# New step tables for the token mixers of a decoder layer, and tail copies on two engines

## The chip, the cores and the metric

The kernel runs on one core of a Trainium2 chip. Its engines work side by side, each through its own list of instructions in order: TensorE (PE in the profile, its weight loads PEld), VectorE (DVE), ScalarE (ACT), GpSimd (POOL) and SyncE (SP), which issues the DMAs here. The metric is the device time of one execution in microseconds. Before the change it is 2779.05 us, the median of three runs (2774.12, 2779.05 and 2781.64).

## The reference

One decoder layer on 2048 tokens of width 1024, in float32. An input projection feeds two groups of token mixers, and the rest is an output projection, a squared-ReLU MLP and a gated embedding:

```python
proj = jnp.einsum('btd,dc->btc', rms_norm(h, pre_mix_norm), w_in)
qkv = jax.nn.silu(causal_depthwise_conv(qkv, gdn_conv))          # q, k, v of 4 heads
o_a = gated_delta_rule_chunked(l2norm(q_a), l2norm(k_a), v_a, g_dec, beta)
o_a = gated_head_norm(o_a, gdn_norm, z_gdn)
o_b = hgrn2_chunked(jax.nn.silu(q_hg), k_b, i_hg, log_f)         # 4 more heads
o_b = gated_head_norm(o_b, hgrn_norm, g_hg)
h = h + rms_norm(concat(o_a, o_b) @ w_out, post_mix_norm)
y = jnp.square(jax.nn.relu(rms_norm(h, pre_mlp_norm) @ w_mlp_up)) @ w_mlp_down
h = h + rms_norm(y, post_mlp_norm)
e = rms_norm(p @ w_ple_proj, ple_norm)
h = h + e * jax.nn.sigmoid(h @ w_ple_gate)
```

Inside the gated delta rule each chunk needs a triangular system solved: with k the keys and decay the running gates, `a_mat = I + strict_lower((beta k) k^T * decay)`, then `u = a_mat^-1 (beta v)` and `w = a_mat^-1 (beta k exp(gc))`. The state runs from chunk to chunk.

## The kernel before

The 2048 tokens are cut into four quarters of 512. Large products are done as three float32r products of a split into a high and a low part, so one output tile of the input projection is 24 matmuls of 128x512.

**Works and steps.** The mixer stage (about 46 to 1136 us) is a list of 132 works: in each quarter one work for the decay inputs (`ab`) and 8 per head for 4 heads (k, q, v and z of the delta rule, then f, i, q and g of HGRN2). A work is 24 matmuls and is cut into three steps of 8. After each step `tick()` runs one piece of every mixer whose turn it is: a mixer is a generator, and a table of offsets (`A_STEPS` for the delta rule, `B_STEPS` for HGRN2, `A_LAST` and `B_LAST` for the very last head) says at which steps after its head's start each of its pieces, from `yield` to `yield`, is emitted. A head starts every 24 steps and its mixers take some 60, so the pieces of two or three heads lie between the matmuls of a third.

**What sets the order.** On TensorE and SyncE the order is the order of emission (`manual_schedule`). On VectorE, ScalarE and GpSimd a scheduler orders the instructions when the program is built. All engines take their lists in order, and wait for each other by semaphores. A work's split weights are kept in DRAM in quarter 0 and reloaded by SyncE in the later quarters; the reload waits until TensorE has left the buffer, which ties SyncE's place to TensorE's.

**The delta rule's pieces** (`gdn_mixer`), in their order: the decays' load (`gf`); their exponentials (`e`); the keys turned, their squares summed (`ssk`, L598) and `ktail`; the root (L602, on GpSimd); the scales `cc`, `ncc`, `inv` (L606); the products `kk` (L621, L622), the system `u` (L625), `qk`, and the keys and queries scaled by the decays (L629 to L631); the values turned, and the store of the system, `ud` (L641, four DMAs); its load in another layout, `sys` (L650), with the off-diagonal blocks (`um`); the inverse of the 32-wide blocks by substitution in eight pieces on VectorE (L656 to L666); its store `xd` and load `xt` (L671, L678); a transpose on VectorE (`xn`, L680); the combination to 128 wide (`psp`, `psx`, `pst`, `psd`, L685); then the recurrence, three pieces for each of four chunks: `psa` (L727) and `r` (L729), `psb` (L732) and `w` (L734), `psc` (L737), the output and the new state `S` (L739). In it TensorE and VectorE alternate from step to step.

**The head's end** (`finish`, `norm_steps`): squares, a sum over partitions on TensorE (`nrm`, L262), that row copied by ScalarE (L265) and stored by SyncE in the same piece (`sd`, L267), loaded again in another layout (L270), scaled and rooted (L272, L158), stored (`rd`, L276), loaded over all partitions (`rsb`, L237), multiplied into `og` (L556) and stored (`mixd`, L558).

**HGRN2's pieces** (`hgrn_mixer`): elementwise products, six levels (L801 to L829; each with products `at`, masked copies and scaled queries and keys), and a recurrence of four chunks (L841 to L845).

**Between the quarters** `decays` turns the work `ab` into decays (L462 to L486, with transposes `ps_gb` at L482), `load_x` loads, scales and splits the next quarter's x (L943 to L959), and `down_sums` (L979 to L990) prepares sums of MLP weights on VectorE.

**The tail.** When the works are done, at about 1088 us, 16 tiles of the embedding's projection (`embed_tile`, 6 matmuls each, `mme`) fill TensorE between the last mixers' pieces. Each tile lies in one of two banks of `pm`; ScalarE copies it (`e`, L299) and squares it (`sq_e`, L225), VectorE adds the squares (L226), SyncE stores the copy (L301).

## Time and profile before

| | us |
|---|---|
| median of three runs | 2779.05 |
| the profiled execution | 2779.64 |
| its span, first to last instruction | 2777.8 |
| TensorE busy | 2694.8 (97%) |
| VectorE busy | 2045.8 (74%) |
| ScalarE busy | 1470.1 (53%) |
| TensorE's granted clock | 0.994 |

In the stretch from 140 to 560 us TensorE is busy for 406.04 of 420 us and VectorE for 326.16; from 1050 to 1135 us for 76.33 and 65.55 of 85 us. In a row of a group, the number behind the bar is the busy time, then the mean of one instruction in ns, then the idle time just before the group's instructions with what ended it. In a row of the waits stand who waited for whom, the total in us, the number of times, and the longest. A row of the timeline has the start, the duration, engine, line and operation, and in brackets the idle time before it. SPq is SyncE's queue of DMA issues. Quarters and heads are counted from 0.

### The profile page before, as it was taken

What the parts mean: (1) busy time and instruction counts of PE and PEld (TensorE: products, weight loads), DVE (VectorE), ACT (ScalarE), POOL (GpSimd) and SP (SyncE); (2) the same over time, 40 slices, a digit from 0 to 9 for tenths busy, and PEclk for the clock granted to TensorE, in tenths of its full rate; (3) what the DMA queues carried; (4) which work ended last, traced back from release to release, by engine and by line L of the source; (5) the groups of instructions that cost most, each with busy time, mean ns of one, the idle gap of its engine ahead of it and who ended that gap; (6) DMA issues with size and microseconds to landing.
All of it is one profiled execution on the core that took longest, in us unless ns stands there. A gap on an engine that the chain in (4) does not pass through costs nothing.

```text
span 2777.8 us, 38374 instructions
## 1 busy us (share of the span) xinstructions
PE 2694.8 (97%) x12721; PEld 2216.6 (80%) x12721; DVE 2045.8 (74%) x4242; ACT 1470.1 (53%) x2943; POOL 103.8 (4%) x104
## 2 busy tenths in 40 slices
PE   7999999999999999999899999999999999999999
PEld 5788788788888887777688888887888888887887
DVE  6787877777777677577889767857787765567765
ACT  6665555455546445576555546545455445465421
POOL 0000000000000000000000000001000000001000
PEclk9999999999999999999999999999999999999999
DMA  7777777667666665887466447667454356677663
GB/s 261 261 246 221 238 235 245 218 208 252 216 212 201 213 226 169 274 278 256 139 216 221 170 168 245 220 195 237 160 189 153 139 171 204 194 254 242 216 200 122
DMA packets 268598, 589.24 MB, mean 212 GB/s; under 512 B 55642, under 2 KB 59960, under 8 KB 249200
## 3 DMA queue, kind: packets, MB, share of 16 engines
q1 hardware_dynamic: 268400, 586.79, 63.4%
q8 instruction: 101, 1.65, 0.3%
q14 instruction: 97, 0.79, 0.1%
HBM read 419.75 MB, written 166.92 MB: 211 GB/s over the span
## 4 chain that ended last, share of the span: by engine, by line
PE 58%; DVE 13%; DMA 9%; issue 6%; ACT 3%; SPq 1%; POOL 1%; DVEq 0%; POOLq 0%; ACTq 0%
PE u L1091 22%; PE d L1091 19%; PE mm L1023 7%; PE mmg L1091 6%; DVE pr_g L661 2%; DMA ud_g<-u_g 2%; DVE xs_g L664 1%; DMA sys_g<-ud_g 1%; DVE xs_g L666 1%; PE mmo L1091 1%; DMA rd_g<-m_g 1%; DMA da<-sumd 1%; DMA rsb_g<-rd_g 1%; DMA raw_xt<-in_xT_dram 1%; DMA b<-h1d 1%
## 5 line engine op out<-in xcount | busy, mean ns | idle before, releaser
L1023 PE MATMUL mm<-xt,w 128*128 128x512 f32 x3072 | 775.1, 401 | 2.3 <-DVE acc_vg L505 0.8
L1023 PEld LDWEIGHTS mm<-xt,w 128*128 128x128 f32 x3072 | 560.5, 189 | 113.0 <-DVE acc_vg L505 1.3
L1091 PE MATMUL d<-db,da 128*128 128x512 f32 x2688 | 614.1, 390 | 6.3 <-ACT db L215 4.0
L1091 PE MATMUL u<-t,wu 128*128 128x512 f32 x2604 | 608.1, 396 | 3.3 <-ACT wu L162 3.3
L1091 PEld LDWEIGHTS d<-db,da 128*128 128x128 f32 x2688 | 505.1, 188 | 114.6 <-ACT db L215 5.3
L1091 PEld LDWEIGHTS u<-t,wu 128*128 128x128 f32 x2604 | 489.7, 188 | 121.0 <-ACT wu L162 4.1
L216 DVE TENSOR_TENSOR db<-db 128x512 fp32r<-128x512 f32 x224 | 160.5, 717 | 77.0 <-ACT db L215 75.8
L1420 DVE TENSOR_TENSOR u<-u,u 128x512 f32<-128x512 f32 x224 | 150.3, 682 | 73.2 <-PE u L1091 72.0
L215 ACT ACTIVATE db<-db 128x512 fp32r<-128x512 f32 x224 | 140.8, 629 | 86.1 <-DMA db<-hid 84.1
L1091 PE MATMUL mmo<-mixT,w_out 128*128 128x512 f32 x720 | 172.5, 400 | 8.7 <-DVE w_out L163 6.3
L1091 PE MATMUL mmg<-h2T,wg 128*128 128x512 f32 x768 | 178.2, 394 | 0.0
L1461 ACT ACTIVATE u<-u 128x512 f32<-128x512 f32 x128 | 80.9, 632 | 179.0 <-DVE u L1420 178.6
L1091 PEld LDWEIGHTS mmo<-mixT,w_out 128*128 128x128 f32 x720 | 137.1, 191 | 43.1 <-DVE w_out L163 8.1
L1091 PEld LDWEIGHTS mmg<-h2T,wg 128*128 128x128 f32 x768 | 144.4, 188 | 33.5
L163 DVE TENSOR_TENSOR da<-da 128x512 fp32r<-128x512 f32 x128 | 93.8, 732 | 86.9 <-ACT da L162 86.5
L162 ACT ACTIVATE da<-da 128x512 fp32r<-128x512 f32 x128 | 80.4, 628 | 135.3 <-DMA da<-sumd 100.9
L162 ACT ACTIVATE wu<-a 128x512 fp32r<-128x512 f32 x124 | 74.1, 624 | 49.1 <-DMA a<-in_w_up_dram 47.9
L661 DVE TENSOR_TENSOR pr_g<-xs_g,sys_g 128x16 f32<-128x16 f32 (+14 forms) x240 | 93.8, 391 | 5.3
L226 POOL TENSOR_TENSOR acc_y<-acc_y,sq_y 128x512 f32<-128x512 f32 x28 | 38.2, 1363 | 1398.0 <-ACT sq_y L225 1398.0
L163 DVE TENSOR_TENSOR wu<-a,wu 128x512 fp32r<-128x512 f32 x124 | 84.7, 686 | 4.8 <-ACT wu L162 4.6
L1462 ACT ACTIVATE u<-u 128x512 f32<-128x512 f32 x128 | 80.8, 631 | 3.7
L163 DVE TENSOR_TENSOR da<-dr,da 128x512 fp32r<-128x512 f32 x96 | 66.2, 689 | 16.0 <-ACT da L162 13.6
(374 smaller groups left out, 3802.2 us busy)
## 6 DMA issues: line engine op xcount, KB each, us to landing
w<-cache_in SPq DMA_DIRECT2D x96, 1024.0 KB
db<-hid SPq DMA_DIRECT2D x224, 256.0 KB
cache_in<-w SPq DMA_DIRECT2D x32, 1024.0 KB
hid<-u SPq DMA_DIRECT2D x128, 256.0 KB
da<-sumd SPq DMA_DIRECT2D x128, 256.0 KB
a<-in_w_up_dram SPq DMA_DIRECT2D x124, 256.0 KB
hid<-ht SPq DMA_DIRECT2D x96, 256.0 KB
dr<-in_w_down_dram SPq DMA_DIRECT2D x96, 256.0 KB
```

Source lines behind the costliest of these rows:

```text
L162: S.activation(t[:, 0], raw, AF.Copy)
L163: eng.tensor_tensor(t[:, 1], raw, t[:, 0], ALU.subtract)
L215: S.activation(t[:, 0], plain(t), AF.Copy)
L216: V.tensor_tensor(t[:, 1], plain(t), t[:, 0], ALU.subtract)
L226: eng.tensor_tensor(acc, acc, sq, ALU.add)
L661: V.tensor_tensor(pr[:, :, :, 0:i], xs[:, None, :, 0:i].broadcast_to([P, 2, GC, i]), sys[:, 0:i, i : i + 2].rearrange("p j two -> p two j" ...
L664: V.tensor_reduce(xs[:, :, i : i + 2].rearrange("p g two -> p two g"), pr[:, :, :, 0 : i + 1], AX.X, ALU.add)
L1023: PE.matmul(ps, *terms[i], start=i == 0, stop=i == nt - 1)
L1091: PE.matmul(ps, a, b, start=start, stop=stop)
L1420: V.tensor_tensor(c[new], c[old], ps, ALU.add)
L1461: S.activation(c[k], c[k], AF.Relu)
L1462: S.activation(c[k], c[k], AF.Square)
```

## The change

All instructions stay the same in kind and number, but for eight copies that move from ScalarE to VectorE, and two more loads of ScalarE's function tables (70 for 68). The tables of offsets change:

- In `gdn_mixer` the store `ud` gets a piece of its own directly behind `kk`, `u` and the scaled keys; the turned values follow in the next piece. The piece of the root comes two steps behind the squares instead of one. Counted from the head's start, kk goes from step 10 to 11, the store stays at 12, the load `sys` goes from 14 to 15, the inverse from 16 to 17, and everything behind it one step later.
- In `norm_steps` the store `sd` is a piece of its own, one step behind the row's copy. The tables of all callers get one more entry.
- The last head of the first three quarters runs its pieces from the store `xd` on three steps later still; head 0 of quarter 0 runs all its pieces two steps later.
- `load_x` of quarters 2 and 3 starts 16 steps before the quarter instead of 9.
- `decays` has 7 in place of 5 as its fourth offset in quarter 0.
- In the tail `e` is copied by VectorE for odd tiles.

```diff
-A_STEPS = ((3, 6, 7, 8, 9, 10, 12, 14) + tuple(range(16, 24)) + (24, 26, 28, 30, 32, 34, 36)
-           + tuple(range(38, 50)) + (50, 52, 54, 56, 57, 58, 60, 61))
+A_STEPS = ((3, 6, 7, 9, 10, 11, 12, 13, 15) + tuple(range(17, 25)) + (25, 27, 29, 31, 33, 35, 37)
+           + tuple(range(39, 51)) + (51, 53, 54, 56, 58, 59, 61, 63, 64))
-B_STEPS = (24, 26, 28, 30, 32, 34, 36, 38, 40, 42, 43, 44, 45, 46, 48, 50, 52, 53, 54, 56, 57)
+B_STEPS = (24, 26, 28, 30, 32, 34, 36, 38, 40, 42, 43, 44, 45, 46, 48, 49, 51, 53, 54, 56, 58, 59)
-A_LAST = (A_STEPS[:16] + (24, 25, 27, 28, 29, 30, 31) + tuple(range(32, 44))
-          + (44, 46, 48, 49, 50, 51, 53, 54))
-B_LAST = tuple(range(24, 38)) + (39, 41, 42, 43, 44, 46, 47)
+INVERSE = 17
+A_LAST = ((3, 6, 7, 8, 9, 10, 11, 12, 14) + tuple(range(16, 24)) + (24, 25, 27, 28, 29, 30, 31)
+          + tuple(range(32, 44)) + (44, 46, 47, 49, 50, 51, 52, 54, 55))
+B_LAST = tuple(range(24, 38)) + (39, 40, 42, 43, 44, 46, 48, 49)
...
         S.activation(row, ps[0:1, :], AF.Copy)
+        yield
         sd = dr.tile([1, QT], F32, name=f"sd_{name}")
         nc.sync.dma_start(sd, row)
         yield
...
-        S.activation(e, ps, AF.Copy)
+        if turns and d % 2:
+            V.tensor_copy(e, ps)
+        else:
+            S.activation(e, ps, AF.Copy)
...
             yield
-            psv = turned(live.pop("v"), f"v{n}", pp)
-            vt = mt(f"vt_{n}", "vt", 2)
-            S.activation(flat(vt), psv, AF.Copy)
 
             ud = dr.tile([NC, NB, SB, SB], F32, name=f"ud_{n}")
             for b in range(NB):
                 sl = slice(b * SB, (b + 1) * SB)
                 nc.sync.dma_start(ud[:, b].rearrange("c j i -> j c i"), u[sl, :, sl])
+            yield
+            psv = turned(live.pop("v"), f"v{n}", pp)
+            vt = mt(f"vt_{n}", "vt", 2)
+            S.activation(flat(vt), psv, AF.Copy)
             yield
...
+                if h == 3 and q < NQ - 1:
+                    a_steps = a_steps[:INVERSE] + tuple(o + 3 for o in a_steps[INVERSE:])
+                if h == q == 0:
+                    a_steps = tuple(o + 2 for o in a_steps)
...
-            at(per_q * q, load_x(q), range(-9, 0))
+            at(per_q * q, load_x(q), range(-9, 0) if q == 1 else (-16, -14, -12, -10, -8, -6, -3, -2, -1))
...
-               [4 * q + i for i in (0, 2, 4, 5, 6)])
+               [4 * q + i for i in (0, 2, 3, 5, 6, 7)])
...
-                        at(clock[0], decays(ps, q), (0, 2, 4, 5))
+                        at(clock[0], decays(ps, q), (0, 2, 4, 5 if q else 7))
...
-                    new = embed_tile(q, d, ple[d // 4], pts[q], accs, m2, 2)
+                    new = embed_tile(q, d, ple[d // 4], pts[q], accs, m2, 2, True)
...
-                           [1 + i for i in (0, 2, 4, 5, 6)])
+                           [1 + i for i in (0, 2, 3, 5, 6, 7)])
```

Three places show what the tables do to the lists. In the names g1_1 is the delta rule of quarter 1, head 1, h1_0 HGRN2 of quarter 1, head 0; the last number is the buffer's, and it and the line numbers differ between the two programs. The first place is VectorE around the system of head 1 in quarter 1; before, and then after:

```order
L822 TENSOR_TENSOR qk_h1_0_3757<-qk_h1_0_3757,gg_h1_0_3_4248 128x2x8x16
L823 COPY_PREDICATED att_h1_0_4026<-cst_84,at_h1_0_4_4294 128x2x8x16
L818 TENSOR_TENSOR qk_h1_0_3757<-qk_h1_0_3757,gg_h1_0_5_4370 128x2x2x64
L625 SCALAR_TENSOR_TENSOR u_g1_1_4306<-kk_g1_1_0_4308,ncc_g1_1_4196,e_g1_1_3875 128x128 x2
L628 TENSOR_TENSOR qk_g1_1_4307<-kk_g1_1_0_4308,e_g1_1_3875 128x256
L556 SCALAR_TENSOR_TENSOR og_g0_3_3995<-og_g0_3_3995,cols_87,rsb_g0_3_4191 128x512
L625 SCALAR_TENSOR_TENSOR u_g1_1_4306<-kk_g1_1_2_4316,ncc_g1_1_4196,e_g1_1_3875 128x128 x2
L628 TENSOR_TENSOR qk_g1_1_4307<-kk_g1_1_2_4316,e_g1_1_3875 128x256
```

```order
L829 TENSOR_TENSOR qk_h1_0_3730<-qk_h1_0_3730,gg_h1_0_3_4230 128x2x8x16
L830 COPY_PREDICATED att_h1_0_4006<-cst_84,at_h1_0_4_4279 128x2x8x16
L996 TENSOR_TENSOR wd2_0_4164<-wd2_1_4165,wd2_0_4164 128x512
L825 TENSOR_TENSOR qk_h1_0_3730<-qk_h1_0_3730,gg_h1_0_5_4359 128x2x2x64
L997 TENSOR_TENSOR wd2_1_4165<-wd2_1_4165,wd2_0_4164 128x512
L631 SCALAR_TENSOR_TENSOR u_g1_1_4314<-kk_g1_1_0_4316,ncc_g1_1_4187,e_g1_1_3851 128x128 x2
L634 TENSOR_TENSOR qk_g1_1_4315<-kk_g1_1_0_4316,e_g1_1_3851 128x256
L631 SCALAR_TENSOR_TENSOR u_g1_1_4314<-kk_g1_1_2_4324,ncc_g1_1_4187,e_g1_1_3851 128x128 x2
L634 TENSOR_TENSOR qk_g1_1_4315<-kk_g1_1_2_4324,e_g1_1_3851 128x256
```

The output of an earlier head (og_g0_3) no longer stands between the two halves of u, and the weight sums (wd2, down_sums) now stand ahead of u instead of behind it.

The second place is SyncE's queue from a weight reload ahead of the store to the load of the same system; before, and then after:

```order
L183 DMA w_24_1_1_4344<-cache_in25_1634 128x2048
L641 DMA ud_g1_1_4379<-u_g1_1_4306 32x4x32 x4
L431 DMA xs2_2_1_4394<-in_x_dram 128x512
L650 DMA sys_g1_1_4424<-ud_g1_1_4379 128x1x1024
L183 DMA w_28_1_1_4433<-cache_in29_1732 128x2048
```

```order
L185 DMA w_24_1_1_4340<-cache_in25_1614 128x2048
L644 DMA ud_g1_1_4361<-u_g1_1_4314 32x4x32 x4
L239 DMA rsb_g0_3_4376<-rd_g0_3_4305 128x512
L437 DMA xs2_2_1_4392<-in_x_dram 128x512
L185 DMA w_28_1_1_4418<-cache_in29_1712 128x2048
L657 DMA sys_g1_1_4441<-ud_g1_1_4361 128x1x1024
```

The load of the system has moved behind the next weight reload (w_28), and the load of an earlier head's scale (rsb_g0_3) now stands between store and load.

The third place is TensorE early in quarter 1, where the last head of quarter 0 goes on (psp5_g0_3) and the decays of quarter 1 are turned (ps_gb_1); before, and then after:

```order
L1023 MATMUL mm_0_1_0_3400<-xt1_2_3163,w_0_1_0_3235 128x512 x2
L685 MATMUL psp5_g0_3_3413<-xn_g0_3_3307,um5_553 128x128 x2
L816 MATMUL at_h0_3_2_3420<-qk_h0_3_2953,keys_h0_3_1_3369 128x2x64 x2
L482 MATMUL ps_gb_1_3434<-cst_84,gb_1_3314 128x36
L482 MATMUL ps_gb_1_3434<-cst_84,gbb_1_3432 128x36
```

```order
L1034 MATMUL mm_8_1_0_3473<-xt1_5_3194,w_8_1_0_3312 128x512
L692 MATMUL psp5_g0_3_3507<-xn_g0_3_3402,um5_553 128x128 x2
L823 MATMUL at_h0_3_4_3514<-qk_h0_3_2938,keys_h0_3_3_3457 128x2x64 x2
L541 MATMUL t_kg1_0_3529<-cst_84,y_kg1_0_3385 128x128 x4
L1034 MATMUL mm_8_1_0_3473<-xt1_5_3194,w_8_1_0_3312 128x512 x2
```

The piece psp5_g0_3 has gone from the second work of the quarter behind its first step (mm_0) to the third work behind its second (mm_8), four steps later; the transposes ps_gb stay in mm_0, in quarter 1 as in quarter 0.

More of the change, by code (lines that the diff above doesn't have):

```diff
@@ L292, in stage_ple, with embed_tile @@
         return ready
-    def embed_tile(q, d, w, pt, accs, pool, bufs):
+    def embed_tile(q, d, w, pt, accs, pool, bufs, turns=False):
         ps = bank(f"mme_{q}_{d}")
```

## The prediction

> **What bounds the kernel now.** I read the page first, then the waits of TensorE and SyncE's queue, then the timeline around the largest of these waits. The page:
>
> ```profile
> span 2777.8 us, 38374 instructions
> PE 2694.8 (97%) x12721; PEld 2216.6 (80%) x12721; DVE 2045.8 (74%) x4242; ACT 1470.1 (53%) x2943; POOL 103.8 (4%) x104
> L1023 PE MATMUL mm<-xt,w 128*128 128x512 f32 x3072 | 775.1, 401 | 2.3 <-DVE acc_vg L505 0.8
> ```
>
> TensorE is busy for 97% of the span, and the change takes no matmul away. What it can win is idle time of TensorE alone, 2777.8 - 2694.8 = 83 us in all, and of that the part that lies in the mixer stage. The big projection of that stage hardly waits (2.3 us over 3072 matmuls). The waits sit at the small matmuls of the mixers:
>
> ```profile
> PE psb_g L732 <- DVE r_g L729: 16.6, 19, 2.5
> PE mme L189 <- ACT sq_e L225: 12.6, 8, 5.4
> PE psp_g L685 <- DVE xn_g L680: 3.7, 4, 1.6
> PE psa_g L727 <- DVE S_g L739: 3.5, 5, 1.1
> PE ps_gb L482 <- DVE gbb L479: 2.8, 1, 2.8
> PE ps_gb L482 <- DVE gb L472: 1.4, 1, 1.4
> ```
>
> The columns are total us, times, longest. All but the mme rows wait for VectorE, so the question is why VectorE is late. It runs its list in order, and the lists of waits show what holds it and what holds SyncE's queue (140 to 1050 us):
>
> ```profile
> DVE xs_g L666 <- DMA sys_g<-ud_g: 20.2, 8, 3.7
> SPq L650 <- DMA ud_g<-u_g: 48.7, 15, 6.0
> SPq L267 <- ACT osq_h L265: 51.6, 13, 5.0
> SPq L267 <- ACT osq_g L265: 36.1, 14, 4.3
> ```
>
> VectorE stands 20.2 us, in 8 heads, before the first instruction of the triangular inverse, because the system (sys_g) has not come back from DRAM. SyncE in turn stands 48.7 us, in 15 heads, because it may not load the system before its store has landed. One place shows the whole chain, head 3 of quarter 0:
>
> ```profile
> 266.54 2.04 SPq L641 DMA_DIRECT2D ud_g<-u_g  x4
> 273.96 0.53 SPq L650 DMA_DIRECT2D sys_g<-ud_g  x1
> 278.70 0.23 DVE L666 SCALAR_TENSOR_TENSOR xs_g<-xs_g,sys_g 128x4 f32<-128x4 f32 x1 [2.83 <-DMA sys_g<-ud_g]
> 281.32 0.49 PE L727 MATMUL psa_g<-S_g,y_kg 128*128 128x128 f32 x2 [0.81 <-DVE S_g L739]
> 285.06 0.75 DVE L946 SCALAR_TENSOR_TENSOR raw_xt<-raw_xt,cols,rsb_x 128x512 f32<-128x512 f32 x1 [1.03 <-DMA raw_xt<-in_xT_dram]
> 286.13 0.80 PE L732 MATMUL psb_g<-r_g,xt_full 128*128 128x128 f32 x2 [2.47 <-DVE r_g L729]
> ```
>
> The load is issued 7.4 us after the store began and needs 4.7 us to the first use. VectorE loses 2.83 us, the state update of the previous head queued behind it is late, TensorE waits 0.81 us at psa and 2.47 us at the next psb. The second wait has a second cause in front of it, 1.03 us for an x load that SyncE issued behind the blocked system load.
>
> **The change part by part.** I add to the profiled execution's own time, 2779.64 us; the median of the runs is 2779.05, 0.6 below.
>
> *System earlier.* The chain kk, u, store, load, inverse moves by one step as a whole; store and load keep their places in the queue before and behind a weight reload, so what changes is how early u is ready. Head 1 of quarter 1 before:
>
> ```profile
> 400.90 0.61 PE L816 MATMUL at_h<-qk_h,keys_h 128*128 128x128 f32 x4
> 401.35 0.39 PE L621 MATMUL kk_g<-y_kg 128*128 128x128 f32 x2
> 402.91 0.39 PE L622 MATMUL kk_g<-y_qg,y_kg 128*128 128x128 f32 x2
> 404.37 0.74 DVE L556 SCALAR_TENSOR_TENSOR og_g<-og_g,cols,rsb_g 128x512 f32<-128x512 f32 x1
> 405.03 0.60 DVE L625 SCALAR_TENSOR_TENSOR u_g<-kk_g,ncc_g,e_g 128x128 f32<-128x128 f32 x2
> 406.56 3.20 SPq L641 DMA_DIRECT2D ud_g<-u_g  x4
> 414.89 0.53 SPq L650 DMA_DIRECT2D sys_g<-ud_g  x1
> ```
>
> Here kk (401.35 to 403.30) stands behind a level of the other mixer in the same step, and u behind that level's work on VectorE; og_g (0.66 us from start to start) cuts u in two. So u is finished at 405.63, 4.7 us after TensorE reached the step at 400.90. After the change kk's step holds no such level, and og_g stands behind u: kk takes 1.95 us from the step's first instruction and the last pair of u 0.60, together 2.55. That makes u ready 4.7 - 2.55 = 2.2 us earlier against the step that needs it. The mean stall to be covered is 20.2 / 8 = 2.5 us, so most of it goes. The load now stands in the queue behind the next weight reload, so by then the store has landed for the most part, and SyncE no longer stands 48.7 us there; the x load behind it, 1.03 us late above, also comes in time. The new wait is the store's own: it stands one step behind kk, not two, so SyncE stands for u there, about the 2.55 us just worked out, and behind it wait the load of the norm's scale and the loads of x for the square sums, which are needed two steps later.
>
> What TensorE gains: all five psa waits (3.5 us) come right after such a stall, and five psb waits follow in the next step, 1.32, 2.47, 1.03, 1.22 and 1.34, together 7.4 us. The first and a middle pair:
>
> ```profile
> 215.87 0.49 PE L727 MATMUL psa_g<-S_g,y_kg 128*128 128x128 f32 x2 [1.00 <-DVE S_g L739]
> 219.54 0.49 PE L732 MATMUL psb_g<-r_g,xt_full 128*128 128x128 f32 x2 [1.32 <-DVE r_g L729]
> 549.32 0.49 PE L727 MATMUL psa_g<-S_g,y_kg 128*128 128x128 f32 x2 [1.10 <-DVE S_g L739]
> 552.87 0.49 PE L732 MATMUL psb_g<-r_g,xt_full 128*128 128x128 f32 x2 [1.22 <-DVE r_g L729]
> ```
>
> Bounds 0 and -10.9 us. I take three quarters, -8, because 2.2 us of head start covers the mean stall but not the longest (3.7).
>
> *The other psb waits,* 16.6 - 7.4 = 9.2 us in 14 places, have a VectorE that is busy, not stalled. The row sum of a step and its collisions with conv and levels change with the shift, in both directions. VectorE also loses short stalls (a norm's scaling now has two steps behind its squares). Bounds -9 and +5; I take -3.
>
> *Last heads three steps later.* Around the quarter's start the transposed inverse stands behind the decays of the next quarter:
>
> ```profile
> 315.77 0.68 DVE L469 SCALAR_TENSOR_TENSOR sp<-sp,se 4x512 f32<-4x512 f32 x1 [1.70 <-ACT se L468]
> 317.51 1.35 DVE L472 TENSOR_TENSOR_SCAN gb<-one,sp 4x128 f32<-4x128 f32 x4
> 319.25 0.71 PE L685 MATMUL psp_g<-xn_g,um 128*128 128x128 f32 x4 [0.73 <-DVE xn_g L680]
> ```
>
> Four steps more put psp into the next-but-one matmul group, past the scans. Three of the four psp waits are of this kind, 3.7 less the longest, 1.6, which is head 0's: -2.1 us. The head's recurrence then meets the next head as in the other heads: 0, with the bounds above.
>
> *The decays' third step.* The table gives 7 for 5 in quarter 0, but this generator has two yields and ends in its third call, at offset 4. The fourth entry is never used, and the order of TensorE has the transposes where they were. So the 2.8 + 1.4 us of ps_gb stay: 0, where a reader of the diff would book -4.
>
> *Square sums and row stores a step apart; x loads spread; head 0 two steps later.* They take SyncE's stands at L267 (51.6 + 36.1 us) away. SyncE is not the bound, and the projection waits for no weight (2.3 us above, none for DMA): 0 by themselves, counted above through VectorE. Two more table loads on ScalarE, 1.28 us each as below, meet an engine that is 53% busy.
>
> ```profile
> 55.67 1.28 ACT L468 ACT_TABLE_LOAD   x1
> ```
>
> *Tail copies on two engines.* Eight of 16 copies leave ScalarE. Between 1086 and 1137 us:
>
> ```profile
> L189 PE MATMUL mme<-pT,w_pleb 128*128 128x512 f32 x96 | 26.1, 407 | 5.7 <-ACT sq_e L225 4.9 <-ACT acc_e L222 0.8
> L299 ACT ACTIVATE e<-mme 128x512 f32<-128x512 f32 x15 | 8.9, 591 | 2.0 <-PE mme L189 1.0 <-DMA ed<-e 0.9
> L216 DVE TENSOR_TENSOR mixT<-mixT 128x512 fp32r<-128x512 f32 x8 | 5.5, 689 | 4.6 <-ACT mixT L215 4.5
> L1420 DVE TENSOR_TENSOR u<-u,u 128x512 f32<-128x512 f32 x224 | 150.3, 682 | 73.2 <-PE u L1091 72.0
> ```
>
> ScalarE sheds 8 x 0.59 = 4.7 us, and TensorE waits 5.7 us for it. VectorE takes on 8 x 0.68 = 5.5 us by the nearest row that reads a bank (L1420), and it already loses 4.6 us to mixT. The wait changes engines rather than going. Bounds -5 and +10; I take 0.
>
> Sum: -8 - 3 - 2.1 + 0 + 0 = -13 us, 2779.6 - 13 = **2766 us** (0.5%).
>
> **Rivals.** *A: the stalls move, they don't go.* The whole chain is shifted as one, so if kk's step is no emptier in most heads (down_sums puts four tensor operations of 128x512, some 0.68 us each by the row of L1420, before u in head 1 of quarter 1), sys_g is as late as before, and only the psp waits and a few others go: -4, 2775 us. For it: VectorE is 74% busy and SyncE's store now stands for u. Against: og_g and the level leave the step in every head.
>
> *B, slower: the tail's banks.* A bank is read by copy and square. The copy on VectorE now stands in VectorE's queue, and the square on ScalarE behind it. If VectorE is late by its longest mixT stall, 2.2 us (4.6 us in three stalls), plus the copy's 0.68, eight tiles cost up to 8 x 2.9 = 23 us: -13 + 23 = +10, 2790 us. It decides from about 1.7 us per tile, where it eats the gain. Against: two banks give a tile's time of slack, and the 51 us of this window hold 16 tiles (96 matmuls, 6 each), 3.2 us for one. That readers of one bank on two engines run one after the other, this row of the start-up and the mixers shows, where VectorE waits for a copy of ScalarE whose result it does not use:
>
> ```profile
> DVE acc_kg L505 <- ACT hist L502: 4.0, 3, 1.5
> ```
>
> The Trainium skill, "PSUM — Partial Sum Buffer", section "PSUM bank collisions raise a hardware error", says that two engines may not touch one bank and quadrant at once, reads included, and that a scheduler adds a dependency for it. By that rule the split cannot run copy and square side by side, and the trace agrees (4.0 us in three waits).
>
> *C: better.* VectorE, without 20 us of stalls, catches up and most psb waits go: -10.9 - 9 - 2.1 - 2 = -24, 2756 us.
>
> **How the numbers follow.** Forecast 0.50, A 0.32, B 0.10, C 0.08. A measurement of this kernel can tell about 0.3%, 8.3 us. Of the forecast's weight 0.43 lies beyond that, with C's 0.08 and 0.05 of A: faster 0.56. Same: 0.07 of the forecast, 0.25 of A, 0.02 of B: 0.34. Slower: 0.08 of B and 0.02 of A: 0.10. The range runs from C, 2755, to just above the time before, 2781, and leaves out B's upper half.
>
> **What would show it.** Right: the DVE wait for sys_g falls from 20.2 to below 8 us, psa's waits for S_g to about 1, SyncE's stand at the system load to a few us, psp to 1.6, and ps_gb stays near 4.2. Wrong: the sys_g stall stays, or mme waits for DVE copies in the tail by more than 8 us, or psb waits stay near 16 with a VectorE that never idles.

## The result and the profile after

The changed kernel takes 2796.85 us, the median of four runs (2793.7 to 2802.75), beside 2777.61 us of the kernel before. The ratio is 1.0071, 95% interval 1.0049 to 1.0094: **slower by 19 us**, where the prediction had 13 us faster and a range that ended at 2781. Measured a second time it was 1.0067 (1.0046 to 1.0088). The profiled execution took 2793.7 us, 14.1 more than that of before. From here on a ratio is always to the kernel before on the same chip; the profiled executions serve for the places, not for the size, since one of them can lie 5 us or more from its kernel's median.

The page after, with the rows that answer to the first ones of the prediction (new lines stand up to 11 further down, L1023 is L1034, L685 is L692, L680 is L687, L732 is L739, L727 is L734):

```profile
span 2791.9 us, 38379 instructions
PE 2700.7 (97%) x12721; PEld 2214.9 (79%) x12721; DVE 2045.7 (73%) x4250; ACT 1472.3 (53%) x2937; POOL 104.3 (4%) x104
L1034 PE MATMUL mm<-xt,w 128*128 128x512 f32 x3072 | 790.3, 402 | 2.2 <-DVE ssk_g L608 2.2
```

The same work on every engine, and 91 us of idle TensorE instead of 83. The largest waits of TensorE between 46 and 1160 us, total, times, longest:

```profile
PE psa_g L734 <- DVE S_g L746: 8.1, 16, 1.7
PE psp_g L692 <- DVE tail_g L585: 6.4, 3, 3.0
PE psp_g L692 <- DVE xn_g L687: 5.9, 3, 3.7
PE psb_g L739 <- DVE r_g L736: 4.5, 10, 0.7
PE ps_gb L488 <- DVE gbb L485: 2.7, 1, 2.7
```

The psb waits for r_g fell from 16.6 to 4.5, as the prediction wished (6.6 with those for other work of VectorE, smaller rows that are not shown). But psa rose from 3.5 to 8.1 and psp from 3.7 to 12.3. All waits of this view together are 37.6 us before and 43.0 after. SyncE's stand at the load of the system fell as forecast, from 48.7 to 10.4 us (140 to 1050 us). But the stall of VectorE for the system, which was to go (140 to 1060 us; 20.2 in 8 heads before), nearly doubled; the wait for the key squares (jk_g) rose too, from 17.8 us:

```profile
DVE xs_g L673 <- DMA sys_g<-ud_g: 38.7, 12, 4.7
DVE ssk_g L608 <- ACT jk_g L604: 27.0, 13, 3.5
```

By stages of the profiled runs (first big matmul of a quarter to that of the next), quarter 0 is 3.3 us shorter, quarters 1 to 3 are 3.7, 5.6 and 2.3 longer, the tail of the mixers (first tail matmul to the first of the output projection) 3.5 longer, 51.7 for 48.2 us.

### The profile page after: what moved, and what is told of

Same layout as the page of the kernel before. It is cut to its first block, busy times and chain, and to the rows that moved or that the text cites. A ratio compares the mean times of both kernels' runs of the same rounds, so it can differ in the third digit from the quotient of the medians.

```text
span 2791.9 us, 38379 instructions
## 1 busy us (share of the span) xinstructions
PE 2700.7 (97%) x12721; PEld 2214.9 (79%) x12721; DVE 2045.7 (73%) x4250; ACT 1472.3 (53%) x2937; POOL 104.3 (4%) x104
## 4 chain that ended last, share of the span: by engine, by line
PE 47%; DVE 5%; DMA 4%; issue 3%; ACT 2%; SPq 0%; POOL 0%; DVEq 0%; ACTq 0%; POOLq 0%
PE u L1102 22%; PE d L1102 18%; PE mmg L1102 6%; DMA da<-sumd 1%; DMA raw_out<-in_w_out_dram 1%; PE mmo L1102 0%; DMA xo<-in_xT_dram 0%; DMA dr<-in_w_down_dram 0%; DMA h2d<-y 0%; DVE w_out L165 0%; PE mme L191 0%; DVE t L165 0%; DMA mixT<-mixd 0%; DMA b<-h1d 0%; ACT L1138 0%
## 5 line engine op out<-in xcount | busy, mean ns | idle before, releaser
L1034 PE MATMUL mm<-xt,w 128*128 128x512 f32 x3072 | 790.3, 402 | 2.2 <-DVE ssk_g L608 2.2
L1034 PEld LDWEIGHTS mm<-xt,w 128*128 128x128 f32 x3072 | 557.1, 189 | 109.1 <-ACT kt_g L606 2.6
L673 DVE SCALAR_TENSOR_TENSOR xs_g<-xs_g,sys_g 128x4 f32<-128x4 f32 x256 | 57.6, 225 | 45.3 <-DMA sys_g<-ud_g 39.7
```

Of the source, the lines that this page charges most:

```text
L673: V.scalar_tensor_tensor(xs[:, :, i + 1], xs[:, :, i], sys[:, i, i + 1 : i + 2], xs[:, :, i + 1], ALU.mult, ALU.add)
L1034: PE.matmul(ps, *terms[i], start=i == 0, stop=i == nt - 1)
```

## The experiments

### Undoing one part, or moving one suspect

Two theories stood at the start. **Q**: two kinds of load (the system, 512 KB, and the transposed inverse xt, four of 16 KB) now stand in SyncE's queue right behind a 1 MB weight reload, and come late for that. **B**, a rival of the prediction: the tail's copies.

```diff
 # reload behind the work's first step, quarters 1 to 3
-                split_work(j + 2)
+                behind = j + 2 not in staged
+                if not behind:
+                    split_work(j + 2)
 ...
                     tick()
+                    if s == 0 and behind:
+                        split_work(j + 2)
```

> The changed kernel, but in quarters 1 to 3 the 1 MB weight reload of a work is issued behind the DMAs of the work's first step instead of ahead of them. Theory Q (queue place): the change pushed the system's load (and the load xt) directly behind the reload; issue to first use went from about 4.6 us to 7.3 us, and VectorE's waits for sys_g from 20 to 39 us. Then with the load ahead of the reload, issue to use returns to about 4.6 us, the sys_g stall falls below 12 us, and the time falls by 6 to 12 us, to 2785 to 2791 us. Rival D (VectorE's new collisions, the tail and the last heads): the sys_g stall may fall, but the time stays at 2794 to 2800 us.

Measured: 1.0042 (1.0029 to 1.0055), some 8 us better than the change, though the two intervals overlap at their ends. The stall for the system fell from 38.7 to 19.9 us. What the queue looked like in the kernel before and in the changed one, SyncE around one system load of quarter 2:

```profile
681.33 0.53 SPq L650 DMA_DIRECT2D sys_g<-ud_g  x1
681.95 0.54 SPq L183 DMA_DIRECT2D w<-cache_in  x1
```

```profile
685.64 0.32 SPq L185 DMA_DIRECT2D w<-cache_in  x1
686.14 0.54 SPq L657 DMA_DIRECT2D sys_g<-ud_g  x1
```

The prediction had seen that the load moves behind the reload and took it for harmless, because the store would have landed by then. The store has indeed landed by then (the 10.4 us above). But where VectorE waits for the load in quarters 1 to 3, it takes 6.7 to 9.3 us from issue to first use after the change, where it took 4.6 to 5.1 before. The edit did not bring this back, as Q had said it would: in this run it is 7.6 to 10.0 us. Another reload still goes out 1.0 to 2.1 us ahead of the load (0.5 to 2.9 in the changed kernel, 5.9 to 10.7 in the one before). The stall is smaller because the load is issued earlier against its use. So a load close behind a reload does come late, but this run did not take it away from there; what the stall is worth is shown further below.

```diff
-                    new = embed_tile(q, d, ple[d // 4], pts[q], accs, m2, 2, True)
+                    new = embed_tile(q, d, ple[d // 4], pts[q], accs, m2, 2)
```

> The changed kernel, but the tail's copies all on ScalarE again, as before the change. From the first tail tile to the first output matmul the changed kernel took 51.7 us against 48.2. Theory Q: the tail is a separate loss of about 3.5 us, so 2793 us, and the mixer quarters keep their extra 8 us. Rival T (the tail is the main loss through banks and VectorE's order): 2780 to 2786 us. If the copies on two engines help and other things lengthened the tail, the time rises to 2798 to 2802 us.

Measured: 1.0040 (1.0028 to 1.0051), some 9 us better; the tail is 45.7 us instead of 51.7, and the waits of psp and mme in it, 7.6 us together, are gone; one of 4.9 us at at_h takes the place of a part of them.

```diff
 # in the kernel before
-A_STEPS = ((3, 6, 7, 8, 9, 10, 12, 14) + ...
+A_STEPS = ((3, 6, 7, 8, 9, 10, 12, 15) + ...
```

> The kernel before, with one entry of the delta rule's table changed from 14 to 15: the load of the system is issued one step later, which puts it behind the next weight reload; nothing else in the tables moves, the inverse stays at step 16. Theory Q: issue to first use grows from 4.6 to above 7 us, VectorE's stall for sys_g from 20 to 45 to 60 us, and the time by 6 to 14 us, to 2784 to 2792 us. Rival D: the load is hidden for the most part, the time stays within 3 us of 2778 us.

Measured: 1.0069 (1.0057 to 1.0081), as much as the whole change, but at another place than Q said. The system's stall hardly moved (21.6 us); TensorE waited for the transposed inverse instead:

```profile
PE psp_g L685 <- DVE xn_g L680: 19.5, 4, 7.6
```

One step of delay in one load of the chain is passed on to its end, and there psp has no slack (spare time before its data is late). The four waits, of 3.9 to 7.6 us, are at head 0 of quarter 0 and at heads 3 of quarters 0 to 2: the same four places at which psp waited 0.7 to 1.6 us before. That the prediction had not looked for: it booked three of these waits as 2.1 us to be won, and did not read them as a sign that no spare time stands behind them.

```diff
-                if h == 3 and q < NQ - 1:
-                    a_steps = a_steps[:INVERSE] + tuple(o + 3 for o in a_steps[INVERSE:])
```

> The changed kernel without the three later steps of the last heads of quarters 0 to 2. In the changed kernel their psp waits 1.7, 3.0 and 1.7 us for VectorE at the new place, against 0.7 to 0.8 us at the old one. Theory Q: with the shift the load xt stands behind a reload as well and xn is ready only 61 to 66 us after kk's step, against 54 to 57 before; without it the time falls by 2 to 5 us, to 2792 us. Rival S (the shift does what it is made for, and the loss lies elsewhere): the time stays or rises to 2800 us.

Measured: 1.0025 (1.0017 to 1.0034): the shift of heads 3 is the largest part of the loss, some 12 us.

### Do the three losses add?

The edits above, put together: heads 3, tail and reload; then heads 3 and tail alone.

> The changed kernel with three parts taken back together: the shift of heads 3, the tail copies on VectorE, and (not in the change, but what it made worse) the weight reload ahead of the system load; the rest of the change stays. Same outputs. One by one these gave about -12.4 us (heads 3), -8.7 (tail copies) and -7.6 (reload), each against the changed kernel at 1.0071 of the time before. Theory 1, three separate losses: they add, 1.0071 x 2774 - 28.7 = 2765 us, 0.997 of the time before: what is left of the change, an earlier system with the load ahead of the reload, then gains some 9 us, near the -8 that I predicted for it. The stall of VectorE for the system is under 20 us, the wait of TensorE for the inverse of heads 3 behind tail_g is gone, the tail is back at 46 to 48 us. Theory 2, one loss seen three times (each of the three only gives VectorE room for the same late work): they do not add, the sum is no better than the best of them, 2778 to 2782, ratio 1.002 to 1.003.

> The changed kernel with the shift of heads 3 and the tail copies on VectorE taken back; the reload stays ahead of the system load, as in the changed kernel. Same outputs. Theory 1 (separate losses): 1.0071 x 2774 - 12.4 - 8.7 = 2772.6 us, 0.9995 of before, no change; the system stall stays above 25 us as in the kernel without the shift alone (30.5), and the run with the reload behind is some 7 us faster than this one. Theory 2 (one loss): as the kernel without the shift alone, 2781, and the reload makes no difference to it.

Measured: 1.0011 (1.0002 to 1.0021) with the reload behind, 1.0002 (0.9992 to 1.0011) with it ahead. Heads 3 and the tail add up (19 of the 21 us expected), and they are the whole loss. The reload adds nothing to them, though the system's stall is 20.7 us with it and 33.0 without: **Q is refuted as a price.** VectorE's stall for the system is real, and TensorE does not pay for it here.

### The tail and heads 3 alone, in the kernel before

> The kernel before with one part of the change alone: every second copy of the embedding's tail on VectorE. Same outputs. If the copies cost in the tail itself (rival B of the prediction, smaller): +3 to +9 us, ratio 1.001 to 1.003, the stretch from the first tail matmul to the first of the output stage longer than its 48.2 us by 3 to 6. If their cost in the changed kernel came only because the head before was late: 0, the stretch 48 us.

Measured: 1.0009 (0.9997 to 1.0020). Alone, the copies cost 0 to 5 us; the tail grew by 1.4 us. In the changed kernel they cost 6 to 9 us. That the rest comes with the new order of the last head is likely, but the intervals do not separate it.

```diff
 # in the kernel before
+                if h == 3 and q < NQ - 1:
+                    a_steps = a_steps[:16] + tuple(o + 4 for o in a_steps[16:])
```

> The kernel before with one part of the change alone: heads 3 of quarters 0 to 2 do all from the inverse's store on four steps later (four, so that they stand where the changed kernel has them: the change has one step for all and three for these heads). Same outputs. By the prediction's term: -2, and the three psp waits around the quarter's start go. Theory Q (the transposed inverse's load, at a step that is a multiple of three, stands right behind a 1 MB weight reload whose issue waits for TensorE, and the head's recurrence meets the next head): +8 to +14 us, ratio 1.003 to 1.005, psp waits for tail_g or xn_g at head 3 of 5 us or more in all, and psa or psb waits longer. If the loss in the changed kernel comes only of the shift together with the other moves: within 3 us of before.

Measured: 1.0067 (1.0055 to 1.0079), +18.6 us for the part that was booked at -2.1. The size is beyond Q's, and the profile shows why. VectorE ahead of the transpose xn at the start of quarter 1, in this run:

```profile
330.27 0.69 DVE L984 TENSOR_TENSOR wd<-wd,wd 128x512 f32<-128x512 f32 x1 [1.81 <-DMA wd<-in_w_down_dram]
...
332.21 0.68 DVE L985 TENSOR_TENSOR wd<-wd 128x512 f32<-128x512 f32 x1
...
333.47 0.68 DVE L987 TENSOR_TENSOR wd<-wd,wd 128x512 f32<-128x512 f32 x1
...
336.09 0.69 DVE L988 TENSOR_TENSOR wd<-wd,wd 128x512 f32<-128x512 f32 x1
336.69 0.42 DVE L818 TENSOR_TENSOR qk_h<-qk_h,gg_h 128x256 f32<-128x256 f32 x1
337.02 0.44 DVE L680 STREAM_TRANSPOSE xn_g<-xt_g 128x256 f32<-128x256 f32 x1
```

xt was issued from 327.04 to 329.31, and VectorE does not idle for it. xn stands behind the first down projection weights (wd) of the quarter, which the scheduler put first, and behind the wait for their load. TensorE stands for it, and is then given a slower clock (columns: busy times, granted clock third from the end):

```profile
337.62 0.86 PE L685 MATMUL psp_g<-xn_g,um 128*128 128x128 f32 x4 [4.88 <-DVE tail_g L579]
330.00:340.00 10.00, 5.12 (x25) 4.31 (x25) 8.00 (x18) 3.67 (x9) 1.01 (x1) 0.90 0.79 268
340.00:350.00 10.00, 10.00 (x56) 8.69 (x56) 5.37 (x19) 7.95 (x30) 1.01 (x1) 0.93 0.50 158
```

0.10 and 0.07 of ten us each are 1.7 us more. There are three such waits in the run (14.2 us in all, longest 5.2), and the clock behind the other two costs the same (0.88 and 0.95 from 600 to 620 us, 0.83 from 870 to 880). Waits and clock are 14.2 + 3 x 1.7 = 19.3 us; less the 2.1 us that psp waited at these heads before, 17.2, beside 18.6 measured.

### Is it VectorE's list?

A new theory, **L**: in the changed kernel too xn is late because it stands behind wd and the conv of the queries in VectorE's list, not because xt lands late.

```diff
 # xt of heads 3 two steps later, the rest three
-                    a_steps = a_steps[:INVERSE] + tuple(o + 3 for o in a_steps[INVERSE:])
+                    a_steps = a_steps[:INVERSE] + tuple(o + (2 if k == 1 else 3) for k, o in enumerate(a_steps[INVERSE:]))
 # and, apart from it: the first wd of a quarter seven steps later
-            at(t, down_sums(g), (0, 4, 6, 10))
+            at(t, down_sums(g), (7, 10, 11, 13) if t % per_q == 5 else (0, 4, 6, 10))
```

> The changed kernel, with one step moved: for heads 3 the load of the transposed inverse (xt) comes two steps later instead of three, the rest of these heads three as in the change. It is then issued one step ahead of the next weight reload and not right behind it, and the scheduler of VectorE, which knows that, puts the transpose xn in front of the four operations on the down projection's weights (wd) and the conv of the queries instead of behind them. Same outputs. Theory L (TensorE's wait at psp of heads 3 comes from the place of xn in VectorE's list, behind wd): the three psp waits of 1.7, 3.0 and 1.7 us at the quarter's start go, and with them the drop of the granted clock behind the longest (1.7 us): -7 to -12 us against the changed kernel, ratio 1.003 to 1.0045. Theory Q (the load's landing is late): the same. Theory S (the shift costs because the whole recurrence of head 3 now meets head 0's chain): no change, 1.006 to 1.008, psa and psp waits later in the quarter as in the changed kernel.

> The changed kernel, with one piece of other work moved: the first weights of the down projection that a quarter loads and sums (wd, four operations of 128x512 on VectorE, 0.69 us each) come 7 steps later, so they are out of the way of head 3's transpose xn at the quarter's start; the load of xt keeps its place behind the reload. Same outputs. Theory L (VectorE's list): the psp waits of heads 3 fall from 6.4 to under 2 us, -5 to -10 us, ratio 1.0035 to 1.0055. Theory Q (the load behind the reload lands late): xn moves up in the list, but then waits there for the load on VectorE, and psp still waits 1.5 us or more in each of the three heads; 1.006 to 1.008.

Measured: 1.0054 (1.0033 to 1.0075) for the earlier xt. That is above L's range, and its interval holds both L's range in part and the changed kernel; the three psp waits are gone in its profile, so they alone are not shown to be the price. For the later wd 1.0029 (1.0016 to 1.0041), 10 us better than the change beside it, a little more than L had said: as good as no shift of heads 3 at all. Changed kernel, then this one, at the start of quarter 1:

```profile
326.18 0.67 DVE L997 TENSOR_TENSOR wd<-wd,wd 128x512 f32<-128x512 f32 x1
...
327.85 0.42 DVE L687 STREAM_TRANSPOSE xn_g<-xt_g 128x256 f32<-128x256 f32 x1
328.42 0.68 PE L692 MATMUL psp_g<-xn_g,um 128*128 128x128 f32 x4 [1.70 <-DVE tail_g L585]
```

```profile
325.89 0.44 DVE L687 STREAM_TRANSPOSE xn_g<-xt_g 128x256 f32<-128x256 f32 x1
327.70 0.61 PE L692 MATMUL psp_g<-xn_g,um 128*128 128x128 f32 x4
```

xt kept its place behind the reload, and xn did not wait for it. L holds for the place of the loss. The same move also removed the psa waits at the next head (1.69 and 1.24 us), so the 10 us are not psp's alone.

The changed kernel beside these, once more:

> The changed kernel itself, once more, beside the three others and the kernel before, so that the differences to it are of one chip. 1.0049 to 1.0094 was measured; the same is expected, 1.006 to 1.0085. If it comes out under 1.004, the parts measured against it were priced too high.

Measured: 1.0067, as said above.

### The decays' third step, really moved

In the changed kernel with heads 3 and the tail taken back:

```diff
-                        at(clock[0], decays(ps, q), (0, 2, 4, 5 if q else 7))
+                        at(clock[0], decays(ps, q), (0, 2, 4 if q else 7))
```

> The changed kernel with the shift of heads 3 and the tail copies taken back (with these two back it was 1.0002 of before), and with the decays' third step of quarter 0 really moved: the entry that is used (the third) is 7 instead of 4, so the transposes to ps_gb come three steps later. Same outputs. The two ps_gb waits, 4.2 us together, are followed by a stretch of 10 us with a granted clock of 0.66 to 0.83, 1.7 to 3.4 us more. If both go and head 0, which is two steps later already, does not wait for the decays instead: 0 to -7 us, 2772 to 2779, ratio 0.9977 to 1.0; if the wait comes back at head 0's first use of the decays' columns: 1.000 to 1.002 with a new wait of 2 us or more before 90 us.

Measured: 1.0002 (0.9989 to 1.0015), no change. The ps_gb waits are gone, and head 0's psp pays, later (at 129.75 us) than expected; it waited 1.3 us without this edit:

```profile
PE psp_g L692 <- DVE xn_g L687: 5.4, 1, 5.4
```

### Where did the predicted gain go?

The first part alone, in the kernel before, then with the reload behind:

```diff
 # ud's stores and a yield ahead of the turned values, and a step table with one more entry
-A_STEPS = ((3, 6, 7, 8, 9, 10, 12, 14) + tuple(range(16, 24)) + (24, 26, ...
-           + tuple(range(38, 50)) + (50, 52, 54, 56, 57, 58, 60, 61))
+A_STEPS = ((3, 6, 7, 9, 10, 11, 12, 13, 15) + tuple(range(17, 25)) + (25, 27, ...
+           + tuple(range(39, 51)) + (51, 53, 55, 57, 58, 59, 61, 62))
```

> The kernel before with only the first part of the change: the system is stored in the same step as the scaled keys, ahead of the turned values, and the delta rule's later steps stand one step later. No shift of heads 3, no other part. Same outputs. The prediction's term: -8, or -11 with the other psb waits, ratio 0.996 to 0.997. Theory A (the stalls move, they don't go: the list of TensorE's waits kept its total, some 35 us, in the kernels with heads 3 and the tail taken back): within 4 us, 0.9986 to 1.0014, psb waits down by 7 us or more and psa, at_h and psp waits up by about as much. Theory Q (the load now stands right behind the reload, issue to use 7 us or more): VectorE's stall for the system stays above 25 us.

> The kernel above, the system alone stored earlier, with the weight reload moved behind the first tick of its work, so that the system's load is issued ahead of it as in the kernel before. Same outputs. Theory Q alone: the system's stall falls under 15 us and the -8 comes: ratio 0.996 to 0.998, and 3 to 8 us faster than the kernel above. Theory A: the stall falls and the time does not follow: within 3 us of the kernel above.

Measured: 1.0100 (1.0083 to 1.0116) and 1.0094 (1.0077 to 1.0112). The core of the change, booked at -8 to -11 us, **costs 28 us alone**, and no theory had that. What it wanted came in part: the psb waits for r_g fell from 16.6 to 6.3 us. TensorE's other waits tell the price, in the first of the two kernels:

```profile
PE psp_g L686 <- DVE xn_g L681: 15.9, 7, 9.0
PE psp_g L686 <- DVE m_g L272: 4.6, 1, 4.6
PE nrm_g L263 <- DVE hl_g L163: 4.2, 6, 2.2
```

One of them from the beginning, in head 1 of quarter 1:

```profile
386.82 0.32 SPq L183 DMA_DIRECT2D w<-cache_in  x1
395.83 0.32 SPq L672 DMA_DIRECT2D xd_g<-xs_g  x1
396.56 0.24 SPq L267 DMA_DIRECT2D sd_g<-osq_g  x1
...
398.30 0.78 SPq L183 DMA_DIRECT2D w<-cache_in  x1
399.18 1.14 SPq L237 DMA_DIRECT2D rsb_h<-rd_h  x1
400.42 3.02 SPq L679 DMA_DIRECT2D xt_g<-xd_g  x4
407.66 0.75 DVE L556 SCALAR_TENSOR_TENSOR og_h<-og_h,cols,rsb_h 128x512 f32<-128x512 f32 x1 [2.78 <-DMA rsb_h<-rd_h]
408.55 0.45 DVE L681 STREAM_TRANSPOSE xn_g<-xt_g 128x256 f32<-128x256 f32 x1
409.15 1.09 PE L686 MATMUL psp_g<-xn_g,um 128*128 128x128 f32 x4 [4.60 <-DVE m_g L272]
```

The inverse ends a step later, SyncE issues nothing from 387.1 to 395.8 and then stores its result (xd; SyncE's stand at this store is 67.0 us from 140 to 1050 us, 20.4 in the kernel before). Behind it come a weight reload and, late together, the norm's scale of the other mixer (rsb_h) and xt; in the kernel before, this head's xt went out at 381.38 us, ahead of the reload at 384.23. VectorE stands 2.78 us for rsb_h, with xn behind it, and TensorE 4.60 us for xn (the row names m_g, but psp reads xn).

All waits of TensorE from 46 to 1160 us are 55.0 us in this kernel, 17.4 more than before. The granted clock is at half in nine stretches of 3.41 us, where it was in two before: up to 12 us more, as the last section works out. Together they account for the 28 us.

The second kernel did not test what it was built for. The system's stall stayed (33.1 us, 32.9 in the first). The psp waits fell from 22.8 us, all rows together, to 12.7, of which 10.6 is one at head 0 of quarter 0; psa rose from 4.3 to 8.2 and at_h from 2.4 to 4.9, all waits came to 52.4 us, and the time hardly moved.

Then the parts were added to it in steps, first the two steps for head 0, then the square sums and row stores a step apart (written as the changed kernel without heads 3, tail copies and spread):

> The kernel before with the system stored earlier and its later steps one step later (which cost +28 us alone) and, in addition, the first head of quarter 0 two more steps later, as in the change. Same outputs. In the kernel without this, that head's psp waited 9.0 us for a transpose which stands in VectorE's list behind a split of weights that wait for their load, and the granted clock was 0.80 and 0.52 in the next two stretches of 10 us, 6.8 us more. If the two steps are there to avoid that: -9 to -16 us against it, ratio 1.004 to 1.007, quarter 0 at 255 to 258 us instead of 265.4. If the wait moves to another head: 1.008 to 1.010.

> The changed kernel with the shift of heads 3, the tail copies and the spread of the x loads taken back: what is left is the earlier system, the first head two steps later and the square sums and scales a step apart. Same outputs. With the spread it was 1.0002 [0.9992, 1.0011]. If the spread does nothing, as I predicted: 0.999 to 1.0015. If it keeps the queue of SyncE free before the quarter's start: slower by 3 us or more, the waits at the end of quarters 1 and 2 longer.

Measured: 1.0088 (1.0075 to 1.0102) and 0.9995 (0.9986 to 1.0004). With what was measured above this makes a ladder from the kernel before to the changed one:

| what it holds of the change | ratio | interval |
|---|---|---|
| the system earlier, later steps one step later | 1.0100 | 1.0083 to 1.0116 |
| + head 0 two steps later | 1.0088 | 1.0075 to 1.0102 |
| + square sums and row stores a step apart | 0.9995 | 0.9986 to 1.0004 |
| + x loads spread | 1.0002 | 0.9992 to 1.0011 |
| + tail copies on two engines | 1.0025 | 1.0017 to 1.0034 |
| + heads 3 three steps later | 1.0071 | 1.0049 to 1.0094 |

The second step is not told apart from nothing by its intervals, though the 9.0 us wait of head 0 fell to 1.45 with it. The third is 26 us, 0.0093 of 2773, larger than anything but the first step. With it all waits of TensorE fall from 48.5 to 28.3 us, psp waits for no m_g any more and nrm_g waits 1.2 us, not 3.1. SyncE's stand at the store of a head's output (mixd) falls from 86.5 to 25.3 us (36.1 before), but VectorE's stall for the norms' scales rises from 19.4 to 27.5, so which of the moved places makes the 26 us is not shown. Two cautions: the first two kernels end a head by my own table (51, 53, 55, ...), not by the change's, so part of the 26 us may be those places, and 6.6 us of it lie in the tail (51.2 and 44.6 us long), where the last head's tables differ as well. And VectorE's list is ordered anew by the scheduler in every kernel, so a step of the ladder is the price of an edit with all that it reorders.

### A better kernel?

The changed kernel with wd later and the tail on ScalarE, then also the reload behind:

> The changed kernel with the quarter's first down projection weights 7 steps later (which gave -10.5 us) and the tail copies back on ScalarE (-8.7). Same outputs. If the two losses are separate and complete: 1.0067 - 0.0038 - 0.0031, 0.9985 to 1.001, 2769 to 2776 beside a kernel before of 2773, the tail at 43 to 47 us, no psp wait above 1 us at the quarter's start. If it is faster than before by over 0.3%, the change with these two repairs is a better kernel.

> The kernel above with the reload behind the first tick of its work as well. Same outputs. Theory A: within 3 us of the kernel above (with heads 3 taken back the reload made no difference, 1.0011 against 1.0002). Theory Q: another -5 to -8 us, 0.996 to 0.998, the stall for the system below 15 us.

Measured: 1.0002 (0.9991 to 1.0012) and 1.0031 (1.0020 to 1.0042). Both losses repaired, the change is level with the kernel before, by another way than taking heads 3 back. The reload behind now costs 8 us, where it gained 8 in the plain changed kernel; neither theory had that, and the system's stall fell to 20.3 us from 33.2, not below 15. In the plain changed kernel it freed psp of heads 3 (their waits are under 1 us in its profile); here these were free already. What its own cost is, no run shows. None of the kernels beats the one before by more than can be measured.

## Why the prediction was wrong

**What bounds the kernel** was right: idle TensorE in the mixers, VectorE late. The working then priced the waits that stood there, and not the slack of the instructions that did not wait.

**System earlier, -8.** The step that failed: "the chain kk, u, store, load, inverse moves by one step as a whole". The chain does not end with the inverse. xd, xt, xn, psp and the norms' steps moved with it, and met other work on VectorE and SyncE. Its head start was sized at 2.2 us for u; the price of the rest was left at nothing, and the part alone measured +28 us, which the other parts then had to gain back. The working says both that store and load "keep their places in the queue" and that the load "now stands in the queue behind the next weight reload"; the second is so, and the landing there was not priced: 6.7 to 9.3 us from issue to use. So the stall that was to fall below 8 us became 38.7. Yet TensorE gained nothing where this stall shrank (from 33.0 to 20.7 us and from 33.2 to 20.3 with the reload behind, in the kernels with heads 3 or wd and the tail mended). So the chain from stall to psa to psb, on which the -8 stood, was read from where both occur together, and did not hold as a price: in the changed kernel psb fell by 10 us (the -3 booked for the other psb waits is in this), while psa, psp and at_h rose by 18.

**Square sums a step apart, x loads spread, head 0 later: 0.** Right for the x loads, and head 0 is not told apart from 0. For the square sums and row stores the 0 was wrong by 26 us, next to the earlier system. The reason given, "SyncE is not the bound", does not make SyncE's places free: the ladder shows that they are not, but not by which wait. Nor did the stands at the row store go: 87.7 us before, 61.4 after, those for osq_h unchanged (51.6 and 51.4).

**Last heads three steps later, -2.1.** This term failed outright. "Past the scans" is what happened, and into the next thing: wd and the conv of the queries. Measured +12 us in the changed kernel, of which moving wd gave 10 back. The view that it quoted, VectorE from 315 to 320 us, ended too early: in the kernel before the four wd operations run from 327.97 to 333.6, behind xn at 318.79, and the shift let them pass it.

**Tail copies, 0 with -5 to +10.** The size lay inside the bounds: 6 us (1.0002 to 1.0025). The place was only half right. The sign "mme waits for DVE copies" never showed; psp stood 3.65 us for an xn that followed a copy and other work of the tail in VectorE's list, and mme 3.9 us for ScalarE's squares:

```profile
1108.33 0.68 DVE L303 COPY e<-mme 128x512 f32<-128x512 f32 x1
1109.74 0.69 DVE L218 TENSOR_TENSOR mixT<-mixT 128x512 fp32r<-128x512 f32 x1 [0.73 <-ACT mixT L217]
1110.35 0.68 DVE L165 TENSOR_TENSOR hl_g<-osq_g,hl_g 128x512 fp32r<-128x512 f32 x1
1110.95 0.69 DVE L228 TENSOR_TENSOR acc_e<-acc_e,sq_e 128x512 f32<-128x512 f32 x1
1111.55 0.44 DVE L687 STREAM_TRANSPOSE xn_g<-xt_g 128x256 f32<-128x256 f32 x1
1112.05 0.71 PE L692 MATMUL psp_g<-xn_g,um 128*128 128x128 f32 x4 [3.65 <-DVE xn_g L687]
```

**The decays' third step: 0** was right: the ps_gb waits stayed (2.7 and 0.8 us). Moved in earnest, they turn into a psp wait, so there was nothing to gain either.

So the loss of 19 us is heads 3 and the tail, and the gain that should have stood against it came to nothing: what is left of the change without these two is 1.0002.

**The rivals.** A, the stalls move, is nearest to what the parts without heads 3 and the tail do together (1.0002). B had the sign but not the mechanism. No rival had a later step of the chain losing its slack, which is where the waits of the loss stand.

## What to carry to other kernels

When a chain is moved by a step, follow it to its end and read the slack of every instruction that moves, the ones that hardly wait now above all: a wait of 0.7 us says that there is none. In an order as tight as this, with the system alone moved, psp cost 19 us more, twice what psb gave. Read VectorE's list in the order that the change gives it ahead of each moved instruction that TensorE needs, and count what a scheduler puts in front. And price parts by adding them one at a time: here a loss of 28 and a gain of 26 hid in a change whose parts seemed small.

## What the runs showed of the chip

A wait of TensorE can be paid twice. In all traces of this case the granted clock is either full or half, and from 46 to 1160 us it falls to half for 3.41 us at a time, 1.7 us more where TensorE is busy. Stretches of 10 us that hold or follow such a wait, of the kernel before (wait 2.47 us at 286), of the changed one (3.03 us at 599.6), and of the one with the system alone (9.0 us at 134.9), with the granted clock third from the end:

```profile
280.00:290.00 10.00, 6.71 (x27) 5.22 (x26) 8.62 (x29) 2.17 (x5) 0.00 (x0) 0.83 0.72 226
```

```profile
600.00:610.00 10.00, 10.00 (x50) 8.47 (x50) 3.73 (x15) 9.78 (x35) 2.01 (x2) 0.83 0.69 246
```

```profile
130.00:140.00 10.00, 5.12 (x17) 4.46 (x18) 1.92 (x4) 5.42 (x21) 0.79 (x1) 0.52 0.92 307
```

0.17 of 10 us is 1.7 us on top of a wait of 2.5 to 3 us. The length of the wait alone does not decide. The stretches of 3.41 us follow each other without a gap, and what counts is how long TensorE stands within one of them. A wait of 1.81 us, ending at 285.4 us in the kernel before with heads 3 later, lay in one stretch, and the next was at half clock. One of 3.54 us, ending at 399.92 in the kernel with the system and head 0 moved, lay across two, and none was (behind the length stands TensorE's busy time):

```profile
283.37:286.78 3.41, 1.60 (x9) 1.17 (x8) 3.20 (x20) 0.66 (x2) 0.00 (x0) 1.00 1.00 256
286.78:290.19 3.41, 2.04 (x6) 1.13 (x5) 2.62 (x8) 0.61 (x1) 0.00 (x0) 0.50 0.82 315
```

```profile
394.77:398.19 3.42, 1.61 (x7) 0.96 (x6) 1.73 (x5) 1.47 (x3) 0.00 (x0) 1.00 0.79 260
398.19:401.60 3.41, 1.68 (x12) 1.59 (x13) 1.25 (x3) 1.63 (x7) 1.01 (x1) 1.00 0.88 227
401.60:405.01 3.41, 3.41 (x18) 2.86 (x17) 1.08 (x7) 3.41 (x17) 1.01 (x1) 1.00 1.00 398
```

Over all these traces, from 46 to 1150 us, every stretch at full clock with 1.9 us or more of idle TensorE was followed by one at half clock, none with less than 1.5 us was, and between the two some were. The Trainium skill, "TensorE: Matmul & The Clock Gate", section "What's actually happening", puts the fall to half clock behind an idle window of about 3.4 us; the length of the stretches agrees, but in these runs a stretch need not be idle from end to end. The prediction priced each wait at its face.

The second is the load close behind the reload, in quarters 1 to 3 and where VectorE waited for it: 4.6 to 5.1 us from issue to use where the last 1 MB on the same queue was issued 5.9 to 10.7 us earlier (kernel before), 6.7 to 9.3 where it was 0.5 to 2.9 us earlier (changed kernel).
